# A fourth product-saving inner pair in each gate and up group, hidden tiles split by accumulating DMAs, products in written order

## The chip, the core and the metric

The kernel runs on one core of one Trainium2 chip. The metric is the time of one execution in microseconds (us), measured on the device; a smaller one is better. Short names of the engines: PE is the matrix engine (PEld its weight loads), DVE the vector engine, ACT the scalar engine, POOL the general engine that here only issues transfers, SP the engine that issues the weight loads.

## The reference

One block of a hybrid encoder for 256 rows of width 2048, all in float32: a mixing layer of four groups, a cross attention over 256 memory rows, and a SwiGLU layer. The change is in the last.

```
x = x + mix @ w_out
x = x + cross_attention(rms_norm(x, norm_g[1]), mem_n, w_xq, w_xkv, w_xo)
gate, up = jnp.split(rms_norm(x, norm_g[2]) @ w_gate_up, 2, axis=-1)   # 2048 x 11264
x = x + (silu(gate) * up) @ w_down                                     # 5632 x 2048
return rms_norm(x, final_norm_g)
```

## The kernel before

**Products.** A float32 number is kept as a rounded part (high) and the rest (low), and each product of an activation tile and a weight tile takes three matmuls: high by high, high by low, low by high (`part`, lines 433 to 435; each is 128 rows by 128 by 512 columns). All weights lie in memory as one stream of slabs, 128 partitions by 2048 columns, in the order in which they are used.

**The stream.** `Stream` turns slabs into weight tiles. A plain slab gives two halves of 1024 columns; for each half ACT casts it into `wh` (line 135) and DVE subtracts to get `wl` (line 136). The `wh` and `wl` tiles rotate over four buffers, so a half can be cast once PE has finished the half that came four earlier. Raw slabs rotate over three buffers. `_fill` keeps the making a few halves ahead of the use.

**Seven products for eight.** Two inner tiles (a pair `ks`) by two column blocks, for two row halves, are eight products. A slab in `PAIRED` does them in seven (Winograd's scheme), 21 matmuls for 24: the activations' sums stand in tiles `z` (`combine`, made once and used for all groups), the weights' sums are made for each slab in `_sums`. Such a slab comes in four phases of 1024, 512, 1024 and 1024 columns, which serve 2, 1, 2 and 2 products; each phase has a cast (line 159) and a subtraction (line 160). Phases 2 and 3 (counted from 0) also need sums of the slab's columns. A slab in `SUMMED` has part of its sums made by transfers: two loads on SP and an accumulating one on POOL (line 102) fill a tile `two`, and DVE adds twice (line 157). One that is in `PAIRED` alone has DVE add four times.

**Gate and up.** The 22 column blocks of `w_gate_up` are done in eleven groups of a gate and an up block, 512 columns each, with all sixteen inner tiles `h3`. The first group is plain; each of the other ten walks the string `GROUP`, one letter for a slab: N is a plain slab (24 matmuls), S one of seven products. When the last S of a group is done, `mixed` joins the products on DVE and ACT; when the last N is done, `upped` and `up` finish the group: two additions, two multiplications, two transposes on DVE (line 557), and then POOL stores the result to the tensor `hidden` (line 559) and loads it again, turned, as four tiles of 128 by 256 (line 564). The generator `fetch` splits each loaded tile into high (ACT) and low (DVE) for the down product; `split` stands in a fixed place by `keep_place`, and a tile is split some steps after its load.

**Down.** `down` does `w_down` in two passes with plans of their own; `down_end` does the last twelve inner tiles of the last column block, one row half after the other, after four matmuls with the identity (line 1244) have added earlier sums to the second row half.

**Who sets the order.** The source is emitted in program order. Background generators (`Background.poll`) are run between products while a planned DVE backlog `owed` is small, and `drain` emits what is left of one. A scheduler then places each engine's instructions by its own estimate of when they can run, except where `keep_place` ties an instruction to the one ahead of it on its engine. At run time each engine takes its instructions in that order.

Of the kernel before, what the change touches and what calls it, by code (L numbers as in the profile page):

```python
# [14 lines left out]
F32R = mybir.dt.float32r  # L15
# [4 lines left out]
ALU = mybir.AluOpType  # L20
# [3 lines left out]
P = 128  # L24
R = 256
# [16 lines left out]
LATE = 12  # L42

GATE_UP = 1920 // 16 + 8
GROUP = "NNSNSNSN"

DOWN = GATE_UP + 80
PASSES = "NNNNSNNSNNSNNSNNSNNSNN", "NSNSNSNSNSNSNSNSNSNNNN"

PAIRED = {a + i for a, plan in [(GATE_UP + 8 * j, GROUP) for j in range(10)] + [(DOWN, PASSES[0]), (DOWN + 22, PASSES[1])]  # L50
          for i, x in enumerate(plan) if x == "S"}
SUMMED = {i for i in PAIRED if i < DOWN}

LAG, OWED, SOON, FAR = 1.3, 0.9, 0.01, 18.0
V_NG = 0
# [16 lines left out]
class Stream:  # L72
# [21 lines left out]
    def _load(self, n):  # L94
# [3 lines left out]
        if n // 16 + 1 in SUMMED:  # L98
# [4 lines left out]
            self.two.append(t)  # L103
        if n // 16 in SUMMED:
            nc.sync.dma_start(self.raw[:, 0:1536], self.W[n // 16][:, 0:1536])
# [149 lines left out]
class Block:  # L255
# [42 lines left out]
    def split2(self, hi, lo, src):  # L298
        self.nc.scalar.copy(hi, src)
        self.tt(lo, src, hi.bitcast(F32), ALU.subtract)  # L300

    def gap(self, pool, n):

        pool.tile([P, n // 4], F32, name=f"gap{next(self.kept)}")
# [159 lines left out]
    def paired_rows(self, w, cols, slots, sums, plan, mixed, first, ready=None, late=0, before=None, swap=False):  # L464

        st, s, nk = self.st, len(sums), len(slots)  # L470
        rest = [k for k in range(nk) if not any(k in ks for ks, _ in sums)]
        steps = [(c, k) for c in range(2) for k in rest]
        todo, q = iter(sums), {}
        count = {"a0": len(rest) + s, "a1": len(rest) + s, "b0": len(rest) + s, "b1": len(rest)}
        left, total = {}, 0

        def put(name, hi, lo, wh, wl):
            if name not in q:
                for x in [name] if name in count else "1675":
                    q[x] = (self.bank if (name in count) == swap else self.gbank)()  # L480
                    left[x] = count.get(x, s)
            new = left[name] == count.get(name, s)
            left[name] -= 1
            self.part(q[name][:, :], hi, lo, wh, wl, new, left[name] == 0)

        form = lambda t, r: (t[:, r * P:(r + 1) * P], t[:, R + r * P:R + (r + 1) * P])
        n = done = 0
        for i, kind in enumerate(plan):
            if before:
                before(i)  # L490
            if kind == "S":
                ks, z = next(todo)
                a = [form(slots[ks[0]], 0), form(slots[ks[1]], 0), form(slots[ks[1]], 1)]
                hi, lo, x4 = self.forms(z, slots[ks[0]])
                x1, s2, s3 = ((hi[:, i * P:i * P + P], lo[:, i * P:i * P + P]) for i in range(3))
                t = (("5", x1), ("7", s3))
                pairs = iter((("1", a[0]), ("b0", x4), ("a0", a[1]), *(t if st.n // 16 in SUMMED else t[::-1]), ("a1", a[2]), ("6", s2)))
                for parts in st.take_sums(w, ks, cols):
                    for wh, wl in parts:
                        name, (hi, lo) = next(pairs)  # L500
                        put(name, hi, lo, wh, wl)
                        self.bg.poll()
                done += 1
                if done == s:
                    mixed(*(q[i] for i in "1567"))
            else:
                for c, k in steps[n:n + 4]:
                    if ready:
                        ready(k)
                    wh, wl = st.take(w, k, cols[c], 4)  # L510
                    for r in range(2):
                        put("ab"[c] + str(r), *form(slots[k], r), wh, wl)
                        self.bg.poll()
                n += 4
            if first and done == s and n >= len(rest):
                first(q["a0"], q["a1"])
                first = None
        assert n == len(steps) - late and done == s
        return [q["b0"], q["b1"]], rest[len(rest) - late:]
# [527 lines left out]
    def gate_up(self, gp, f, z):  # L1047

        nc = self.nc
        box, g, stored = {}, {}, []  # L1050

        def gate(ps):
            for r in range(2):
                g[r] = gp.tile([P, 512], F32, name=f"g{r}", tag=f"g{r}")
                nc.scalar.activation(g[r], ps[r], AF.Silu, scale=box["col"][:, r:r + 1])

        def up(j, ps, h=None):
            h = h or [gp.tile([P, 512], F32, name="h", tag="h", bufs=2) for _ in range(2)]
            for r in range(2):
                self.stt(h[r], ps[r], box["col"][:, r:r + 1], g[r], ALU.mult, ALU.mult)  # L1060
                self.store_turned(self.ff, 4 * j, r, g[r], h[r])
            stored.append(self.bg.now)

        def mixed(q1, q5, q6, q7):

            g[0], g[1], h[0], h[1] = (gp.tile([P, 512], F32, name=n, tag=n, bufs=b) for n, b in (("g0", 1), ("g1", 1), ("h", 2), ("h", 2)))
            nc.scalar.copy(g[0], q1)
            self.tt(h[0], g[0], q6, ALU.add)
            self.tt(g[1], h[0], q7, ALU.add)
            self.tt(h[0], q5, h[0], ALU.subtract)  # L1070
            self.tt(h[1], q5, g[1], ALU.subtract)

        def gated(*ps):

            for r in range(2):
                self.tt(g[r], g[r], ps[r], ALU.add)
                nc.scalar.activation(g[r], g[r], AF.Silu, scale=box["col"][:, r:r + 1])

        def upped(j, ps):

            for r in range(2):
                self.tt(h[r], h[r], ps[r], ALU.add)
            up(j, h, h)

        h = {}

        def fetch(k0, k1, ahead, pause, wait=0):

            m = {}
            for k in range(k0, k1 + ahead):  # L1090
                if k < k1:
                    while len(stored) <= k // 4:
                        yield
                    m[k] = self.tmp()
                    self.load_turned(m[k], self.ff, k)
                if k >= k0 + ahead:
                    while wait and self.bg.now < stored[(k - ahead) // 4] + wait:
                        yield
                    mark = self.mark()
                    self.split(f[k - ahead], m.pop(k - ahead))  # L1100
                    self.keep_place(mark)
                    self.have = k - ahead + 1
                    yield pause

        def norm():

            mark = self.mark()
            nc.scalar.activation(self.mg[:, 0:1], self.mg[:, 0:1], AF.Silu)
            self.keep_place(mark)
            yield 2.0  # L1110
            self.row_norm(1, box)
            yield

        arrival = lambda: gp.tile([P, R], F32, name="ar", tag="ar", bufs=4)
        last = self.bg.add(self.arrive(self.xf[1], 3, arrival, self.put3, FAR), go=True)
        col = self.bg.add(norm())

        def combined():
            for ks, z in sums:
                yield 3.0  # L1120
                yield from self.combine(z, *(self.h3[k] for k in ks))

        sums = [((2 * i, 2 * i + 1), z[i]) for i in range(GROUP.count("S"))]
        comb = self.bg.add(combined())
        ps = self.gemm_rows("w_gate_up", [0, DFF], self.h3,
                            parts=[(range(8), [0]), (range(8, 12), [0]), (range(12), [1]), (range(12, 16), [0]), (range(12, 16), [1])],
                            before=lambda n: n in (1, 3) and self.bg.drain(self.late if n == 1 else last))
        self.bg.drain(col)
        gate(ps[0])
        up(0, ps[1])  # L1130
        early = self.bg.add(fetch(0, FT - 22, 3, 2.0, 15))
        self.bg.drain(comb)
        for j in range(1, DFF // 512):
            upped(j, self.paired_rows("w_gate_up", [j * 512, DFF + j * 512], self.h3, sums, GROUP, mixed, gated, swap=j % 2 == 0)[0])
        self.bg.drain(early)
        self.fetch = self.bg.add(fetch(FT - 22, FT, 6, SOON))

    def down(self, f, sp):
# [72 lines left out]
    def down_end(self, f, ss, ps, rest, split):  # L1211
# [29 lines left out]
        mark = self.mark()  # L1241
# [7 lines left out]
        for r in range(2):  # L1249
# [4 lines left out]
            for c in range(3):  # L1254
                x = self.half(c, r)
                self.stt(x, x, 0.375, fg[:, c * 512:(c + 1) * 512], ALU.mult, ALU.mult)
        nc.scalar.mul(fg[:, 3 * 512:4 * 512], fg[:, 3 * 512:4 * 512], 0.375)
        for r in range(2):
            for k, wh, wl in held:
                self.part_rows(ps[r], r, f[k], wh, wl, False, k == FT - 1)  # L1260
            norm(ps[r], r)


# [627 lines left out]
```

## Time and profile before

| | |
|---|---|
| time, median of 3 runs | 1438.75 us (1436.18 to 1439.48) |
| the profiled execution | 1435.07 us, span 1433.3 us, granted clock 0.999 |
| busy, share of the span | PE 99%, PEld 82%, DVE 80%, ACT 57%, POOL 16% |
| matmuls | 6589 recorded |
| transfers | 343.79 MB, mean 240 GB/s |

In the page's rows, "L136" is line 136 of the kernel; "wl<-raw,wh 128x1024" gives the tile written, the tiles read and the shape. In the timeline, the first number is the start in us from the span's start, the second the time of the merged instructions, and the bracket behind tells how long the engine had been idle and what ended that.

### The profile page before, as it was taken

The numbers are of one execution on the slowest core, as the hardware profiler recorded it, in microseconds if no ns is written. First come the engines' busy times: TensorE is split into PE (matmuls) and PEld (weight loads), VectorE is DVE, ScalarE is ACT, GpSimd is POOL, SyncE is SP. The second block draws the span as 40 slices with busy tenths as digits, with TensorE's granted clock in tenths as the row PEclk, the third lists the DMA queues.
The fourth block names the chain that finished last, engine by engine and source line by source line (L and its number), as shares of the span: only waits on it lengthen the run. The fifth ranks groups of instructions, "written<-read, shape, count | busy, mean of one in ns | idle before, by whom it ended". The sixth has DMA issues, their size and how long they took to land.

```text
span 1433.3 us, 18652 instructions
## 1 busy us (share of the span) xinstructions
PE 1423.0 (99%) x6589; PEld 1180.7 (82%) x6589; DVE 1146.2 (80%) x1738; ACT 815.2 (57%) x1183; POOL 234.8 (16%) x306
## 2 busy tenths in 40 slices
PE   9999999999999999999999999999999999999997
PEld 8888888888888888888888888888888888888886
DVE  6667868777877767777677888898888888989997
ACT  7556565446645555556554656555555556655655
POOL 0000100013212223531431121122011002000000
PEclk9999999999999999999999999999999999999999
DMA  9876564546667788964986999889999887655554
GB/s 352 299 285 248 205 206 162 175 169 224 202 196 236 234 267 252 274 200 166 289 239 209 286 286 277 278 275 282 294 293 288 268 260 229 219 230 179 193 218 147
DMA packets 73037, 343.79 MB, mean 240 GB/s; under 512 B 10957, under 2 KB 12654, under 8 KB 45168
## 3 DMA queue, kind: packets, MB, share of 16 engines
q1 hardware_dynamic: 54848, 288.98, 57.5%
q0 software_dynamic: 17664, 52.97, 15.8%
q8 instruction: 51, 0.84, 0.2%
q10 hardware_dynamic: 432, 0.66, 0.1%
q14 instruction: 42, 0.34, 0.1%
HBM read 322.12 MB, written 20.45 MB: 239 GB/s over the span
## 4 chain that ended last, share of the span: by engine, by line
PE 97%; DVE 1%; ACT 0%; DMA 0%; issue 0%; SPq 0%; ACTq 0%
PE pg L433 22%; PE pg L434 22%; PE pg L435 22%; PE pm L434 7%; PE pm L435 7%; PE pm L433 7%; PE pg L381 4%; PE pg L382 2%; PE pm L1344 1%; PE pm L1022 1%; PE pm L993 1%; DMA raw<-in_W 0%; PE pm L1753 0%; DVE res L283 0%; PE pm L994 0%
## 5 line engine op out<-in xcount | busy, mean ns | idle before, releaser
L136 DVE TENSOR_TENSOR wl<-raw,wh 128x1024 fp32r<-128x1024 f32 (+1 forms) x413 | 494.8, 1212 | 166.1 <-ACT wh L135 163.2
L135 ACT CAST wh<-raw 128x1024 fp32r<-128x1024 f32 (+1 forms) x413 | 424.5, 1043 | 283.9 <-PE pg L435 196.4
L433 PE MATMUL pg<-wh,act 128*128 128x512 f32 (+1 forms) x1191 | 465.6, 391 | 0.0
L434 PE MATMUL pg<-wl,act 128*128 128x512 f32 (+1 forms) x1191 | 463.9, 389 | 0.4 <-DVE wl L136 0.2
L435 PE MATMUL pg<-wh,act 128*128 128x512 f32 (+1 forms) x1191 | 463.9, 389 | 0.0
L433 PEld LDWEIGHTS pg<-wh,act 128*128 128x128 f32 x1191 | 223.8, 188 | 47.8 <-issue 1.5
L434 PEld LDWEIGHTS pg<-wl,act 128*128 128x128 f32 x1191 | 223.8, 188 | 47.2 <-DVE wl L136 1.3
L435 PEld LDWEIGHTS pg<-wh,act 128*128 128x128 f32 x1191 | 223.7, 188 | 47.2 <-DVE act L283 0.4
L159 ACT CAST wh<-raw 128x1024 fp32r<-128x1024 f32 (+1 forms) x150 | 137.0, 921 | 146.8 <-DVE raw L157 46.4
L160 DVE TENSOR_TENSOR wl<-raw,wh 128x1024 fp32r<-128x1024 f32 (+1 forms) x150 | 156.1, 1061 | 57.0 <-ACT wh L159 56.8
L434 PE MATMUL pm<-wl,act 128*128 128x512 f32 x309 | 120.5, 390 | 0.1
L433 PE MATMUL pm<-wh,act 128*128 128x512 f32 x309 | 120.2, 389 | 0.0
L435 PE MATMUL pm<-wh,act 128*128 128x512 f32 x309 | 120.2, 389 | 0.0
L381 PE MATMUL pg<-act,wh 128*128 128x512 f32 x256 | 90.5, 395 | 0.0
L382 PE MATMUL pg<-act,wl 128*128 128x256 f32 x256 | 71.8, 280 | 0.0
L434 PEld LDWEIGHTS pm<-wl,act 128*128 128x128 f32 x309 | 58.0, 188 | 13.0 <-DVE wl L136 0.6
L433 PEld LDWEIGHTS pm<-wh,act 128*128 128x128 f32 x309 | 58.0, 188 | 12.0
L435 PEld LDWEIGHTS pm<-wh,act 128*128 128x128 f32 x309 | 58.0, 188 | 12.0
L102 POOL DMA_DIRECT2D two<-in_W x30 | 26.6, 887 | 241.2 <-DMA two<-in_W 116.0
L157 DVE TENSOR_TENSOR raw<-raw 128x512 f32<-128x512 f32 x90 | 62.0, 689 | 1.3
L159 ACT CAST wh<-two 128x1024 fp32r<-128x1024 f32 x30 | 31.6, 1052 | 51.1 <-PE pg L435 21.7
L381 PEld LDWEIGHTS pg<-act,wh 128*128 128x128 f32 x256 | 48.1, 188 | 10.5
(375 smaller groups left out, 1821.9 us busy)
## 6 DMA issues: line engine op xcount, KB each, us to landing
raw<-in_W SPq DMA_DIRECT2D x216, 1024.0 KB, 5.6
raw<-in_W SPq DMA_DIRECT2D x30, 768.0 KB, 6.1
two<-in_W SPq DMA_DIRECT2D x60, 256.0 KB, 4.9
two<-in_W POOLq DMA_DIRECT2D x30, 512.0 KB, 9.3
raw<-in_W SPq DMA_DIRECT2D x11, 512.0 KB, 7.6
hidden<-g POOLq DMA_DIRECT2D x22, 256.0 KB, 3.7
tmp<-hidden POOLq DMA_DIRECT2D x44, 128.0 KB, 5.4
features<-tmp POOLq DMA_DIRECT2D x32, 128.0 KB, 5.3
```

What stands on the lines that cost most here:

```text
L102: nc.gpsimd.dma_start(t, W[:, 512:1536], accum_op=ALU.add)
L135: nc.scalar.copy(wh[:, a:b], r[:, a:b])
L136: nc.vector.tensor_tensor(out=wl[:, a:b], in0=r[:, a:b], in1=wh[:, a:b].bitcast(F32), op=ALU.subtract)
L157: nc.vector.tensor_tensor(out=out, in0=a, in1=b, op=ALU.add)
L159: nc.scalar.copy(wh, src)
L160: nc.vector.tensor_tensor(out=wl, in0=src, in1=wh.bitcast(F32), op=ALU.subtract)
L381: self.nc.tensor.matmul(p[:, :], wh, slot[:, :], start=start, stop=False)
L382: self.nc.tensor.matmul(p[:, 0:R], wl, slot[:, 0:R], start=False, stop=stop)
L433: self.nc.tensor.matmul(p, hi, wh, start=start, stop=False)
L434: self.nc.tensor.matmul(p, hi, wl, start=False, stop=False)
L435: self.nc.tensor.matmul(p, lo, wh, start=False, stop=stop)
L993: nc.tensor.matmul(p[:, :], q[d][:, r * P:(r + 1) * P], kt[d][:, :], start=d == 0, stop=False)
```

## The change

1. `GROUP` becomes `NSNSsNSN`: four of the eight slabs of a group are done in seven products, the second, fourth, fifth and seventh. The fifth, `s`, is not in `SUMMED`: its sums are four DVE additions and no transfers. A fourth tile `z3` holds the sums of the fourth pair of activations.
2. `fetch` uses `split_far`: ACT writes the high part and the negated, rounded source into the low part's place, and an accumulating transfer issued by POOL adds the source. DVE has no part in it. The fixed place (`keep_place`) is gone there.
3. In `paired_rows` and at the end of `down_end` the three matmuls of each product are tied to the order in which they are written.

```diff
-GROUP = "NNSNSNSN"
+GROUP = "NSNSsNSN"
...
-          for i, x in enumerate(plan) if x == "S"}
-SUMMED = {i for i in PAIRED if i < DOWN}
+          for i, x in enumerate(plan) if x in "Ss"}
+SUMMED = {GATE_UP + 8 * j + i for j in range(10) for i, x in enumerate(GROUP) if x == "S"}
...
+    def split_far(self, hi, lo, src):
+
+        self.nc.scalar.copy(hi, src)
+        self.nc.scalar.mul(lo, src, -1.0)
+        self.nc.gpsimd.dma_start(lo, src, accum_op=ALU.add)
...
+            mark = self.mark()
             self.part(q[name][:, :], hi, lo, wh, wl, new, left[name] == 0)
+            self.keep_place(mark)
...
-            if kind == "S":
+            if kind in "Ss":
...
-                    mark = self.mark()
-                    self.split(f[k - ahead], m.pop(k - ahead))
-                    self.keep_place(mark)
+                    t = f[k - ahead]
+                    self.split_far(t[:, 0:R], t[:, R:512], m.pop(k - ahead))
...
-        sums = [((2 * i, 2 * i + 1), z[i]) for i in range(GROUP.count("S"))]
+        z = z + [gp.tile([P, 1024], F32R, name="z3")]
+        sums = [((2 * i, 2 * i + 1), z[i]) for i in range(4)]
...
         for r in range(2):
+            mark = self.mark()
             for k, wh, wl in held:
                 self.part_rows(ps[r], r, f[k], wh, wl, False, k == FT - 1)
+            self.keep_place(mark)
             norm(ps[r], r)
```

## The prediction

> **What bounds the kernel now.** I read the page's first and fourth part, and then the windows of the gate and up groups.
>
> ```profile
> span 1433.3 us, 18652 instructions
> PE 1423.0 (99%) x6589; PEld 1180.7 (82%) x6589; DVE 1146.2 (80%) x1738; ACT 815.2 (57%) x1183; POOL 234.8 (16%) x306
> PE 97%; DVE 1%; ACT 0%; DMA 0%; issue 0%; SPq 0%; ACTq 0%
> 976.00:1018.00 42.00, 42.00 (x187) 34.75 (x187) 36.83 (x45) 24.82 (x31) 7.76 (x9) 1.00 0.93 285
> 1018.00:1059.00 41.00, 41.00 (x182) 33.97 (x181) 35.13 (x40) 22.29 (x26) 7.75 (x9) 1.00 0.91 286
> ```
>
> The chain that ended last is PE's for 97%, and in two windows of a group's length PE is busy for every microsecond (42.00 of 42.00, 41.00 of 41.00). So a matmul less is time less, and any gap that the change opens is time more. DVE is busy 35.13 of 41 us: it has room, but little, and what counts is when in a group it has it.
>
> A group runs from the first matmul of its first slab to that of the next group. These are the two ends of one:
>
> ```profile
> 944.10 0.39 PE L433 MATMUL pg<-wh,act 128*128 128x512 f32 x1
> 985.58 0.39 PE L433 MATMUL pm<-wh,act 128*128 128x512 f32 x1
> ```
>
> It takes 985.58 - 944.10 = 41.48 us for five plain slabs of 24 matmuls and three of 21, which is 183, or 0.2267 us each. A plain slab is then 5.44 us, one of seven products 4.76 us, and its phases 1.36, 0.68, 1.36 and 1.36.
>
> **The matmuls removed.** Four plain slabs and four of 21 make 180: 0.68 us less for each of ten groups, 6.8 us in all. The lists of instructions of the two kernels, as built, have these 30 fewer on PE, so that part of the change is certain.
>
> **What it adds to DVE and ACT.** Slab `s` needs four lows where N had two, and four sums of 128x512.
>
> ```profile
> L136 DVE TENSOR_TENSOR wl<-raw,wh 128x1024 fp32r<-128x1024 f32 x80 | 94.7, 1217 | 5.6 <-ACT wh L135 4.5
> L160 DVE TENSOR_TENSOR wl<-raw,wh 128x512 fp32r<-128x512 f32 x24 | 16.4, 685 | 0.0
> 978.14 3.50 DVE L136 TENSOR_TENSOR wl<-raw,wh 128x1024 fp32r<-128x1024 f32 x3 [0.21 <-ACT wh L135]
> 1393.28 2.87 DVE L157 TENSOR_TENSOR raw<-raw 128x512 f32<-128x512 f32 x4
> 1396.06 1.22 DVE L160 TENSOR_TENSOR wl<-raw,wh 128x1024 fp32r<-128x1024 f32 x1
> 1410.45 0.43 DVE L283 TENSOR_TENSOR tmp<-res,tmp 128x256 fp32r<-128x256 f32 x1
> L159 ACT CAST wh<-raw 128x512 fp32r<-128x512 f32 x24 | 14.9, 620 | 11.9 <-PE pm L435 6.2 <-PE pg L435 5.7
> L135 ACT CAST wh<-raw 128x1024 fp32r<-128x1024 f32 x80 | 81.0, 1048 | 33.0 <-DMA raw<-in_W 12.6 <-PE pg L435 6.6 <-PE pm L435 6.1
> ```
>
> Back to back, three lows take 3.50 us, so one adds (3.50 - 1.22) / 2 = 1.14; four sums hold DVE from 1393.28 to 1396.06, 2.78; a 512 low about 0.60 (the spacing of the sums is 0.7). `s` costs DVE 1.14 + 0.60 + 2.78 = 4.5 us a group more, less 4 x 0.43 = 1.7 where four hidden tiles are split without it: 35.1 + 4.5 = 39.6 of 40.8 us at most. By the average it fits. ACT has 22 of 41 us and gets 1.05 + 0.62 for casts and four negated copies; it fits with ease. The sums of the fourth activation pair are made once, about eight DVE instructions of some 0.43 us, 3.4 us, beside the first group; if nothing covered them they would cost those 3.4.
>
> **The order is the trouble.** I walked one group of the changed kernel through the built order of its instructions, each engine taking its own in turn. Time 0 is the first matmul of slab 1 (N). Rows that it rests on:
>
> ```profile
> 989.98 1.30 DVE L557 STREAM_TRANSPOSE g<-h 128x512 f32<-128x512 f32 x2
> 991.20 1.19 DVE L136 TENSOR_TENSOR wl<-raw,wh 128x1024 fp32r<-128x1024 f32 x1
> 993.51 0.39 PE L435 MATMUL pm<-wh,act 128*128 128x512 f32 x1
> 993.98 1.05 ACT L159 CAST wh<-two 128x1024 fp32r<-128x1024 f32 x1 [1.78 <-issue]
> 1394.80 1.05 ACT L159 CAST wh<-raw 128x1024 fp32r<-128x1024 f32 x1 [2.64 <-DVE raw L157]
> ```
>
> DVE is done with the previous group's sums and transposes at 991.20 - 985.58 = 5.62. A cast into a freed buffer starts some 0.2 us after PE has issued past it (993.98 against 993.74, one matmul after 993.51). PE's second matmul of a half, 0.23 in, is the first to need its low.
>
> *Slab 2 (S).* DVE: low of phase 1 until 6.22, a sum 6.82, low of phase 2 (`two`) 8.04; PE wants that at 5.44 + 1.36 + 0.68 + 0.23 = 7.71, so 0.33 lost, and phase 2 ends at 9.17. On ACT the next cast in the order is half 1 of slab 3, ahead of phase 3 of slab 2, and its buffer is the one that phase 1 holds until 7.48. So that cast runs 7.72 to 8.77, phase 3's until 9.73, and DVE's lows follow in the same order: 9.99 and 11.13. PE wanted phase 3 at 9.40 and gets it at 11.15: 1.75 lost, 2.08 in the slab.
>
> *Slab 4 (S).* Here the hidden tiles come in. In the kernel before, a tile is split three tiles after its load. In the built order of the changed one, the four tiles loaded in a group are split in the same group, and ACT takes all four ahead of the cast of phase 2 of slab 4. It waits for their landing:
>
> ```profile
> 990.99 1.57 POOL L559 DMA_DIRECT2D hidden<-g  x2 [7.62 <-DVE g L557]
> 996.56 3.54 POOL L564 DMA_DIRECT2D tmp<-hidden  x4 [4.00 <-DMA hidden<-g]
> tmp<-hidden POOLq DMA_DIRECT2D x23, 128.0 KB, 5.3
> L291 ACT CAST f<-tmp 128x256 fp32r<-128x256 f32 x14 | 5.6, 401 | 0.0
> 1413.79 0.63 ACT L1257 ACTIVATE raw<-raw 128x512 f32<-128x512 f32 x1 [0.58 <-DMA raw<-in_fg]
> ```
>
> The loads start at 996.56 - 985.58 = 10.98, take 5.3, and follow each other by 3.54 / 4 = 0.885: they land at 16.28, 17.17, 18.05, 18.94. ACT writes a high and a negated copy of the last one (0.40 each; a scaled copy costs what a cast does, 0.63 against 0.62 at 128x512) until 19.75, the cast of phase 2 until 20.8, DVE its low until 22.0. With slab 3 from 12.28 to 17.72, PE wanted it at 17.72 + 1.36 + 0.68 + 0.23 = 19.99: 2.06 lost. Slab 4 ends at 24.54 (17.72 + 4.76 + 2.06), slab 5 so at 24.54 + 4.76 + 2.04 + 0.94 = 32.28 with what follows.
>
> *Slab 5 (`s`), right behind an S.* DVE still has lows of slab 4 and of phases 0 and 1, then the four sums 24.82 to 27.6. Phase 2's cast can start after two of them (1394.80 in the row above lies amid its four sums), but its low has to queue behind the fourth: 28.82. PE wanted it at 24.54 + 2.04 + 0.23 = 26.81: 2.04 lost. Half 0 of slab 6 again goes ahead of phase 3, whose low is done at 31.1 where PE wanted it at 30.21: 0.94 lost. From there to the end of the group I find no gap.
>
> Sum of one such group: 2.08 + 2.06 + 2.04 + 0.94 = 7.1 us of gaps. Groups 1 to 6 split four tiles each and get this; group 7 splits two and gets about 6.4 (its last load lands 1.77 earlier, and part of what slab 4 no longer loses is lost at `s`); groups 8 and 9 split none, so `s` alone loses 1.42 + 0.89 (DVE enters it 0.6 us less behind) and slab 2 its 2.08, 4.4 each; group 10, whose splits wait for buffers instead, I put between the two at 6.0. Together 6 x 7.12 + 6.4 + 2 x 4.4 + 6.0 = 63.9.
>
> **The end of the kernel.**
>
> ```profile
> 1408.35 0.28 PE L1244 MATMUL pm<-tmp,identr 128*128 128x256 f32 x1
> 1410.55 0.77 PE L1244 MATMUL pm<-tmp,identr 128*128 128x256 f32 x2
> 1400.00:1434.00 34.00, 24.54 (x108) 19.55 (x106) 23.85 (x50) 15.86 (x29) 0.00 (x0) 0.93 0.43 155
> ```
>
> Now the four identity matmuls stand among others, of which PE runs 13 while the last of their inputs is made (ready at 1410.45 + 0.43). In the changed order those 13 stand behind them: 13 x 0.2267 = 2.95 us later, with DVE's order there the same.
>
> **Transfers added.** 44 accumulating ones of 128 KB on POOL's queue, POOL idle for over 80% of the span. Nothing but the far later down pass waits for them. For scale:
>
> ```profile
> q0 software_dynamic: 5790, 19.59, 28.2%
> hidden<-g POOLq DMA_DIRECT2D x16, 256.0 KB, 3.7
> two<-in_W POOLq DMA_DIRECT2D x23, 512.0 KB, 9.4
> ```
>
> From the window 851.6 to 1184.1, 332.5 us: 0.282 x 332.5 / 19.59 = 4.8 us of all sixteen transfer engines per MB, so four of them some 2.4 us a group. The share of 0.91 would rise to 0.97 at an unchanged group; a group of 48 us covers it. If that cover is gone (rival A), weights could come up to 2.4 us late a group; I take 0. The queue's order puts the `two` of slab 7 behind the four, which wait for ACT: issued at about 19.75 + 2 x 0.885 = 21.5 it lands 9.4 later, at 31, and slab 7 begins at 32.28 + 5.44 = 37.7, so 0 too; without that cover what is late there comes on top.
>
> **Sum.** -6.8 + 63.9 + 2.95 = +60.0. The profiled execution took 1435.07 us, 3.7 under the median of the runs; on the median the forecast is 1438.75 + 60 = 1498.8, say 1498.
>
> **The rivals.** *A, faster: the feed keeps its lead.* DVE has 1 us a group to spare, and if halves are made early enough that both swapped orders cost under 0.68 us a group and the splits nothing, what is left is -6.8 + 2.95: 1434.9. For it speaks the average, against it that four buffers are all there are and the cast of slab 3 ahead of phase 3 has to wait for PE. 5%.
>
> *B: the order costs, the loads don't.* If the hidden tiles land by about 17 (1.9 us earlier than my 18.94), all ten groups lose 4.4: -6.8 + 44 + 2.95 = +40, 1479. Against it stand the row of 996.56 and 5.3 us. 22%. The Trainium skill, DMA: Bandwidth & Descriptors, "Anatomy of one DMA — SWDGE (gpsimd) path", gives about 2.0 us plus the bytes at 436 GB/s: 2.3 us for 128 KB and 2.6 for 256 KB, an estimate by which they land in time and B holds. The trace does not agree: 5.3 and 3.7 us.
>
> *H: half the order costs.* If ACT and DVE catch up between slabs better than I drew it, half of B's 44 remains: -6.8 + 22 + 2.95, 1457. 6%.
>
> *C: the gaps lower the granted clock.* In the row from 1400 to 1434, PE is busy 24.54 of 34 us and the clock is 0.93. At that clock the 408 us of matmuls in ten groups take 31 more: 1529. Against it: PE would still be busy 85% of a group. 5%. The Trainium skill, TensorE: Matmul & The Clock Gate, "Part 1: The HAM clock gate", has the clock fall after an idle window of some 3.4 us. My longest gap is 2.1, so by that rule C does not come.
>
> The forecast keeps 60%.
>
> **How the numbers follow.** Range 1458 to 1522: it holds the forecast with 10 us either way for transfer times (0.5 us of landing in seven groups is 3.5 us, a phase's low one place off in ten groups 6) and the catch-up that I may have missed, and B. It leaves out A, C and most of H, 15%. About 0.2% is what a measurement of this kernel can tell from no change. Faster 0.05 (A), same 0.02 (between A and H, some 0.4 us a group lost), slower 0.93.
>
> **What would show it.** In the profile of the changed kernel, groups 1 to 6 should last about 48 us and 8 and 9 about 45; PE's gaps should sit ahead of L434 in phases 2 and 3 of slabs 2, 4 and 5, ended by `wl` of L160; ACT should be idle ahead of the hidden tiles' copies, ended by the transfer `tmp<-hidden`; DVE's busy time should hardly change. Before the identity matmuls PE should be idle some 3 us more. If the groups last under 41.5 us, my walk through the queues was wrong as a whole; if slab 4 shows no gap but 2 and 5 do, B holds; if the clock in those windows is under 0.98, C.

## The result, and the profile after

The changed kernel takes 1530.67 us (median of six runs, 1527.24 to 1538.47) against 1436.26 us: the ratio is 1.0662, with a 95% interval of 1.0634 to 1.069. That is 94 us more, where 60 were forecast, and outside the range.

The page of the changed kernel, parts 1 and 4:

```profile
span 1533.3 us, 18733 instructions
PE 1464.1 (95%) x6559; PEld 1191.0 (78%) x6559; DVE 1177.8 (77%) x1762; ACT 847.4 (55%) x1249; POOL 273.1 (18%) x350
PE 76%; DVE 9%; DMA 8%; issue 3%; ACT 2%; POOL 2%; SPq 0%; ACTq 0%; POOLq 0%; DVEq 0%
```

PE has the 30 matmuls less, and yet its busy time went up by 41 us and its idle time from 10 to 69. So there are two losses: gaps, and matmuls that last longer. (A matmul ahead of a gap counts as busy for 0.39 us, in a row it takes 0.2267, so a part of each gap counts as busy too.) The chain names DVE, DMA and ACT where it was PE for 97%.

ACT copies `g` once in each group, near the end of its last slab of seven products, so two neighbouring copies are a group apart. Before, all but one of nine such distances are 41.5 to 41.6 us (41.97 the other). After, from its timeline (start, duration):

```profile
868.77 0.58 ACT L1075 COPY g<-pg 128x512 f32<-128x512 f32 x1
920.23 0.58 ACT L1075 COPY g<-pm 128x512 f32<-128x512 f32 x1
...
1120.19 0.58 ACT L1075 COPY g<-pm 128x512 f32<-128x512 f32 x1
1165.92 0.58 ACT L1075 COPY g<-pg 128x512 f32<-128x512 f32 x1
...
1211.65 0.58 ACT L1075 COPY g<-pm 128x512 f32<-128x512 f32 x1
1273.32 0.58 ACT L1075 COPY g<-pg 128x512 f32<-128x512 f32 x1
```

A group that splits four tiles lasts 51.46 us in the first two rows (five such distances: 50.9 to 52.1). The three groups behind these, of which the first splits two tiles and the others none, last 45.72 to 45.73, the last group 61.67. By the place of the copies, the change costs 7.6 us up to the first one, 81.7 in the nine distances and 10.8 behind them, 100.1 in all, which is the difference of the two profiled spans (the medians differ by 94).

One group's middle, the fourth slab, on PE, ACT and POOL:

```profile
1000.40 0.39 PE L441 MATMUL pg<-wh,act 128*128 128x512 f32 x1
1002.72 0.50 PE L439 MATMUL pm<-wh,z 128*128 128x512 f32 x1 [1.93 <-ACT wh L159]
1003.98 0.80 PE L440 MATMUL pm<-wl,z 128*128 128x512 f32 x1 [0.76 <-DVE wl L160]
1004.58 0.63 PE L441 MATMUL pm<-wh,z 128*128 128x512 f32 x1
...
994.81 0.41 ACT L304 CAST f<-tmp 128x256 fp32r<-128x256 f32 x1 [2.58 <-DMA tmp<-hidden]
996.60 0.41 ACT L304 CAST f<-tmp 128x256 fp32r<-128x256 f32 x1 [1.06 <-DMA tmp<-hidden]
999.46 0.41 ACT L304 CAST f<-tmp 128x256 fp32r<-128x256 f32 x1 [1.61 <-DMA tmp<-hidden]
1001.01 0.40 ACT L304 CAST f<-tmp 128x256 fp32r<-128x256 f32 x1 [0.83 <-DMA tmp<-hidden]
1001.64 1.03 ACT L159 CAST wh<-two 128x1024 fp32r<-128x1024 f32 x1
...
990.26 3.53 POOL L572 DMA_DIRECT2D tmp<-hidden  x4 [2.86 <-DMA hidden<-g]
```

Each of the four tiles holds up ACT until its transfer has landed, the cast of phase 2 (1001.64) comes behind the last, and PE, done at 1000.79, starts again at 1002.72. That is the chain that the prediction walked. What it left at 5% is in the last row of PE: 0.63 us instead of 0.39. From there on, the starts are 0.43 us apart instead of 0.2267. Two windows of the same length, the first from that gap on, the second at about the same place of group 7, which has no gap at slab 4 (the columns are length, busy times, then the granted clock, the share of the transfer engines and GB/s):

```profile
1002.00:1016.00 14.00, 11.50 (x34) 8.48 (x35) 11.80 (x13) 8.04 (x10) 1.70 (x2) 0.76 0.90 205
1108.00:1122.00 14.00, 12.34 (x52) 9.30 (x51) 11.07 (x13) 8.86 (x11) 0.88 (x1) 1.00 0.87 287
```

34 matmuls against 52, and a clock of 0.76 against 1.00. PE's timeline has 120 matmuls of 0.60 us or more (108 of them 0.63), in ten stretches of up to 13: six of them behind slab 4 of groups 1 to 6, two in the last group, one in the down pass and one at the end of the kernel. At 0.43 - 0.23 = 0.2 us each they cost 24 us.

### The profile page after: what moved, and what is told of

Its sections match the earlier page's. It is cut to its first block, busy times and chain, and to the rows that moved or that the text cites. A ratio compares the mean times of both kernels' runs of the same rounds, so it can differ in the third digit from the quotient of the medians.

```text
span 1533.3 us, 18733 instructions
## 1 busy us (share of the span) xinstructions
PE 1464.1 (95%) x6559; PEld 1191.0 (78%) x6559; DVE 1177.8 (77%) x1762; ACT 847.4 (55%) x1249; POOL 273.1 (18%) x350
## 4 chain that ended last, share of the span: by engine, by line
PE 76%; DVE 9%; DMA 8%; issue 3%; ACT 2%; POOL 2%; SPq 0%; ACTq 0%; POOLq 0%; DVEq 0%
PE pg L440 18%; PE pg L441 18%; PE pg L439 18%; PE pm L440 4%; PE pm L441 4%; PE pm L439 4%; PE pg L387 4%; DMA tmp<-hidden 3%; DVE wl L136 3%; DVE wl L160 3%; DMA raw<-in_W 2%; PE pg L388 2%; DMA hidden<-g 1%; ACT wh L135 1%; POOL tmp L572 1%
## 5 line engine op out<-in xcount | busy, mean ns | idle before, releaser
L136 DVE TENSOR_TENSOR wl<-raw,wh 128x1024 fp32r<-128x1024 f32 (+1 forms) x393 | 471.8, 1213 | 167.7 <-ACT wh L135 165.9
L135 ACT CAST wh<-raw 128x1024 fp32r<-128x1024 f32 (+1 forms) x393 | 405.9, 1042 | 280.3 <-PE pg L441 199.4
L440 PE MATMUL pg<-wl,act 128*128 128x512 f32 (+1 forms) x1166 | 457.1, 392 | 8.5 <-DVE wl L160 8.2
L439 PE MATMUL pg<-wh,act 128*128 128x512 f32 (+1 forms) x1166 | 458.3, 393 | 2.1 <-ACT wh L159 1.9
L441 PE MATMUL pg<-wh,act 128*128 128x512 f32 (+1 forms) x1166 | 455.7, 391 | 0.0
L439 PEld LDWEIGHTS pg<-wh,act 128*128 128x128 f32 x1166 | 220.2, 189 | 52.4 <-ACT wh L159 5.1
L159 ACT CAST wh<-raw 128x1024 fp32r<-128x1024 f32 (+1 forms) x190 | 173.8, 923 | 155.1 <-PE pg L441 68.3
L160 DVE TENSOR_TENSOR wl<-raw,wh 128x1024 fp32r<-128x1024 f32 (+1 forms) x190 | 199.1, 1064 | 76.2 <-ACT wh L159 76.0
L441 PEld LDWEIGHTS pg<-wh,act 128*128 128x128 f32 x1166 | 220.1, 189 | 46.0 <-DVE act L283 0.2
L440 PE MATMUL pm<-wl,act 128*128 128x512 f32 x284 | 115.4, 406 | 14.8 <-DVE wl L160 14.8
L439 PE MATMUL pm<-wh,act 128*128 128x512 f32 x284 | 114.7, 404 | 7.4 <-ACT wh L159 7.2
L441 PE MATMUL pm<-wh,act 128*128 128x512 f32 x284 | 113.5, 400 | 0.0
L157 DVE TENSOR_TENSOR raw<-raw 128x512 f32<-128x512 f32 x130 | 89.6, 689 | 2.3
L439 PEld LDWEIGHTS pm<-wh,act 128*128 128x128 f32 x284 | 55.3, 195 | 23.6 <-ACT wh L159 12.0
L441 PEld LDWEIGHTS pm<-wh,act 128*128 128x128 f32 x284 | 55.3, 195 | 11.3
L160 DVE TENSOR_TENSOR wl<-two,wh 128x1024 fp32r<-128x1024 f32 x30 | 36.7, 1224 | 31.8 <-ACT wh L159 31.8
```

What stands on the lines that cost most here:

```text
L135: nc.scalar.copy(wh[:, a:b], r[:, a:b])
L136: nc.vector.tensor_tensor(out=wl[:, a:b], in0=r[:, a:b], in1=wh[:, a:b].bitcast(F32), op=ALU.subtract)
L157: nc.vector.tensor_tensor(out=out, in0=a, in1=b, op=ALU.add)
L159: nc.scalar.copy(wh, src)
L160: nc.vector.tensor_tensor(out=wl, in0=src, in1=wh.bitcast(F32), op=ALU.subtract)
L439: self.nc.tensor.matmul(p, hi, wh, start=start, stop=False)
```

## The experiments

All times are medians in us, beside the kernel before as measured together with them. Distances of two copies of `g` are called group lengths.

**e1, e2, e3: the three parts one at a time.** e1 has the ties of the products alone, e2 the far split alone, e3 the fourth slab alone:

```diff
 e1, on the kernel before
+            mark = self.mark()
             self.part(q[name][:, :], hi, lo, wh, wl, new, left[name] == 0)
+            self.keep_place(mark)
 (and the same around the loop over held)
 e2, on the kernel before
-                    self.split(f[k - ahead], m.pop(k - ahead))
+                    self.split_far(t[:, 0:R], t[:, R:512], m.pop(k - ahead))
 (without its mark and keep_place)
 e3, on the kernel before
-GROUP = "NNSNSNSN"
+GROUP = "NSNSsNSN"
 (with SUMMED, z3 and sums as in the change)
```

> Only the third part of the change: products tied to their written order, the four-slab pattern and the DVE splits as before. Theory Q (the loss is in the queues of ACT and DVE: halves and hidden tiles stand there in an order that PE has to wait for, and a long wait then also lowers the granted clock): the order of ACT and DVE is that of the kernel before, so only the end of the kernel changes, 13 matmuls behind the identity ones: +3 us. Rival O (PE lost the freedom to fill its gaps with other products' matmuls): +20 us or more, with gaps in the gate and up groups.

Measured 1443.79 against 1435.28, ratio 1.0053 (1.0038 to 1.0068): +8 to +9. Theory Q said 3, rival O 20. Some 5 us of it are at the end of the kernel or in the down pass, 2.6 in the groups (the nine distances sum to 376.5 for 373.9).

> Only the second part of the change: hidden tiles split by ACT and an accumulating transfer, three slabs of seven products as before. Theory Q: the tiles loaded in a group are split in the same group, and ACT takes the first one ahead of the halves of the fourth slab; it lands 16.3 us into the group, the halves are wanted at 15.6, so PE waits some 3 us in each of seven groups, and the clock falls behind the wait as in the changed kernel (13 matmuls at 0.43 instead of 0.23 us, 2.6 us): +30 to +45 us. Rival L (the fourth slab's load on DVE is what costs, the far split relieves it): within 3 us of the kernel before, or faster.

Measured 1490.45, ratio 1.0381 (1.0364 to 1.0399): +55. Rival L falls. Theory Q's mechanism is there, but not as regularly as it said: at the fourth slab PE waits 1.2 to 6.2 us in five groups, not seven, and the clock falls in three of them; the size was 10 us over the expected range. PE and ACT of e2, where the fourth slab begins:

```profile
931.42 0.51 PE L439 MATMUL pm<-wh,act 128*128 128x512 f32 x1 [1.92 <-ACT wh L135]
...
930.01 0.40 ACT L304 CAST f<-tmp 128x256 fp32r<-128x256 f32 x1 [3.85 <-DMA tmp<-hidden]
930.33 1.99 ACT L135 CAST wh<-raw 128x1024 fp32r<-128x1024 f32 x2
```

ACT waits 3.85 us for one tile's landing, and the plain half that PE wants stands behind it. Of the 55 us, 37 are in the nine distances (410.8 for 373.9) and 15 behind them; around the end of the last group, where the late tiles' splits stand, PE has gaps of 4.99, 3.37 and 3.06 us.

> Only the first part of the change: four slabs of seven products, hidden tiles split by DVE in a fixed place as before. Theory Q: the second and fifth slab lose 1.4 and 1.0 to 1.6 us a group as in the changed kernel, 24 to 30 us in all, the fourth slab loses nothing, the granted clock stays at 1.00 in the groups; minus 6.8 for the matmuls; the 20 splits come in a crowd at the end of the groups, some 10 us: +27 to +35 us. Rival L: DVE has more to do than in the changed kernel, the groups are no shorter than there: +90 us or more.

Measured 1474.43, ratio 1.0267 (1.0252 to 1.0283): +39. Its groups last 43.7 to 45.1 us. One of them, and PE behind the last one:

```profile
1076.23:1119.89 43.66, 42.63 (x182) 33.31 (x181) 39.37 (x46) 24.33 (x28) 4.21 (x5) 1.00 0.86 257
...
1227.65 0.79 PE L439 MATMUL pg<-wh,f 128*128 128x512 f32 x1 [11.32 <-ACT f L291]
```

DVE is busy 39.4 us of it, more than the kernel before's 35 to 37, but 4 less than the group lasts; the granted clock is 1.00. Theory Q's 2.4 to 3 us a group over the 40.8 of 180 matmuls are there in the last six distances (43.7 to 43.8). Its crowd of splits is, too: of the early 22 tiles the first alone is split in a group, the others stand behind the last one, and PE waits 11.32 us for them at one go; the whole is 4 us over the expected range. Rival L, by its number, falls. The three parts alone sum to 103 us where together they are 94. That the two are near does not show that the parts are independent: the later runs price the same part very differently beside different others.

**e4: gaps by themselves.** Behind the last product of the kernel before stand bursts of 60 matmuls; between two of them ACT copies a tile 0 to 12 times onto itself, and the next burst's first matmul reads it.

```diff
+        for gaps in plan:
+            p = self.bank()
+            for i in range(60):
+                nc.tensor.matmul(p[:, :], (first if i == 0 else a[2])[:, 0:P], a[3][:, :], start=i == 0, stop=i == 59)
+            for g, k in enumerate(gaps):
+                if g:
+                    p = self.bank()
+                    nc.tensor.matmul(p[:, :], a[0][:, 0:P], a[3][:, :], start=True, stop=True)
+                nc.scalar.mul(a[0][:, 0:R], p[:, 0:R], 0.0)
+                for _ in range(k):
+                    nc.scalar.copy(a[0][:, 0:R], a[0][:, 0:R].bitcast(F32))
+            first = a[0]
```

> The kernel before, and behind its last product 55 bursts of 60 matmuls of 128x512, parted by gaps of 0.7 to about 6 us that a chain of ACT copies makes; the last 15 gaps have one matmul amid them. It adds work that the reference does not have. Theory G (a gap by its length lowers the granted clock): bursts behind gaps under a bound run at 0.227 us a matmul throughout, those behind longer ones start with some 13 at 0.43, and the bound lies between 1.4 and 1.9 us. Rival P (the clock fell for another reason, the load of the chip around it): the bursts' speed does not go by the gap ahead of them.

A burst takes 13.9 us, or it takes 15.1 to 16.8, with 5 to 14 matmuls at the lower clock. None of the 18 bursts behind a gap of 1.41 us or less is of the longer kind, 10 of 17 behind gaps of 1.83 to 3.15 us are, and all 9 behind gaps of 4.0 us or more (where one matmul stands amid a gap, its longer part is counted). So rival P falls. Theory G holds for long and short gaps, but its bound is no line. Two bursts behind equal gaps of 1.84 us, the first with the fall and the second without; then two neighbouring windows around each of the two gaps:

```profile
1739.46 0.50 PE L625 MATMUL pm<-act,act 128*128 128x512 f32 x1 [1.84 <-ACT act L632]
1816.31 0.50 PE L625 MATMUL pm<-act,act 128*128 128x512 f32 x1 [1.84 <-ACT act L632]
...
1736.98:1740.39 3.41, 1.57 (x7) 0.98 (x6) 0.00 (x0) 1.60 (x4) 0.00 (x0) 1.00 0.01 2
1740.41:1743.80 3.39, 3.39 (x10) 2.61 (x9) 0.00 (x0) 0.00 (x0) 0.00 (x0) 0.50 0.02 5
1812.08:1815.49 3.41, 2.39 (x11) 1.65 (x9) 0.00 (x0) 0.86 (x3) 0.00 (x0) 1.00 0.00 0
1815.50:1818.90 3.40, 2.59 (x11) 2.17 (x12) 0.00 (x0) 0.73 (x2) 0.00 (x0) 1.00 0.00 0
```

What parts them is the place of the gap. The trace records the granted clock, and all 20 falls in e4 begin at whole multiples of 3.413 us from one another. The windows are such stretches of 3.41 us. The first gap lies in one of them, PE is idle for 1.84 us of it, and the next one runs at 0.50. The second gap is parted by a boundary into 1.02 and 0.82 us, and the clock stays at 1.00. The last section has the count for all runs.

**e5 to e8: the splits in place, the halves in order.** The kernels differ in three things:

```diff
 e5, on the changed kernel
+                    mark = self.mark()
                     self.split_far(t[:, 0:R], t[:, R:512], m.pop(k - ahead))
+                    self.keep_place(mark)
 (and the generator of the early tiles is stepped ahead of slabs 1, 3, 5 and 7)
 e6, on e5: casts, sums and subtractions of the halves in gate and up
+            self.keep_place(mark)
 e7, on e6: the ties of the third part taken out
 e8, on e7
-                    self.split_far(t[:, 0:R], t[:, R:512], m.pop(k - ahead))
+                    self.split(f[k - ahead], m.pop(k - ahead))
```

> The changed kernel, but the hidden tiles' splits (by ACT and an accumulating transfer, as in the change) are tied to a fixed place, one ahead of every second slab, each three tiles after its load. Theory Q: ACT has no landing to wait for, slab 4's wait goes and with it the fall of the clock, groups that split tiles last what groups 8 and 9 of the changed kernel do (45.7 us), group 10 too, the end of the kernel stays: 10 x 4.2 + some 6 = +45 to +52 us against the kernel before, clock 1.00 in the groups. Rival W (ACT's second writing and the accumulating transfers cost by their work, wherever they stand): +80 us or more.

Measured 1508.16, ratio 1.0495 (1.0479 to 1.051): +72. In the groups theory Q holds: they last 44.4 to 47.1 us, the last one 45.73, with no fall of the clock. But 34 of the 72 us lie behind the last copy of `g` (283.1 us for 249.2), where the changed kernel has 10.8; neither theory expected that. PE of e5, in the down pass:

```profile
1277.07 0.80 PE L441 MATMUL pg<-wh,act 128*128 128x512 f32 x1 [5.78 <-DMA act<-tmp]
```

There a tile is split just ahead of its use, and the low part's accumulating transfer is on the path.

> As e5, and in gate and up the casts and subtractions of the weight halves are tied to the order in which they are written, so that half 1 of the next slab no longer goes ahead of phase 3. Theory Q: slab 2's loss of 2.3 us a group goes, slab 5's 2.4 stays in the main, as it comes from the four sums: groups 43 to 43.5 us, +22 to +30 us. Rival S (the sums of `s` are all that counts, the order nothing): as e5.

Measured 1503.17, ratio 1.0463 (1.0433 to 1.0492): +67. The nine distances sum to 409.3 where e5's sum to 410.8, so by its total rival S holds, and the 22 to 30 us of theory Q are far off. The single groups say more. Groups 9 and 10, without splits and at full clock in both, last 44.0 us for e5's 45.7. PE in group 10, four gaps of e5 and then two of e6:

```profile
1196.20 0.50 PE L439 MATMUL pm<-wh,act 128*128 128x512 f32 x1 [0.46 <-ACT wh L159]
1197.65 0.50 PE L440 MATMUL pm<-wl,act 128*128 128x512 f32 x1 [0.95 <-DVE wl L160]
1212.85 0.50 PE L440 MATMUL pg<-wl,z 128*128 128x512 f32 x1 [0.93 <-DVE wl L160]
1215.11 0.50 PE L440 MATMUL pm<-wl,act 128*128 128x512 f32 x1 [0.61 <-DVE wl L160]
...
1199.87 0.50 PE L447 MATMUL pg<-wl,z 128*128 128x512 f32 x1 [1.10 <-DVE wl L164]
1216.44 0.50 PE L447 MATMUL pg<-wl,z 128*128 128x512 f32 x1 [0.93 <-DVE wl L164]
```

With the halves in order, the waits at phase 3 of slabs 2 and 5 (1196.20, 1197.65, 1215.11) are gone; in slab 2 the low of phase 2 comes 1.10 us late instead. That is worth 1.7 us a group, where theory Q said 2.3. It is lost again in groups 7 and 8, in which e6 has a fall of the clock that e5 hasn't (47.8 and 47.3 us for 46.0 and 45.7). The stretch ahead of the first of them, and the next one:

```profile
1076.32:1079.73 3.41, 1.50 (x6) 0.72 (x5) 3.29 (x5) 2.28 (x3) 0.00 (x0) 1.00 0.99 360
1079.74:1083.14 3.40, 3.40 (x9) 2.63 (x10) 3.40 (x4) 2.74 (x3) 0.87 (x1) 0.50 0.59 87
```

No gap there is over 0.97 us, but two of them (0.97 and 0.94) lie in one stretch, 1.91 us of idle time together.

> As e6, but without the third part of the change: the matmuls of a product aren't tied to their order, nor those at the end. Theory Q with what e1 showed (the tie costs 8 us where there is little else to wait for): 8 to 12 us less than e6, +12 to +20 us against the kernel before.

Measured 1493.14, ratio 1.0395 (1.0376 to 1.0414): +57, 10 less than e6. As expected from the tie; the level is e6's.

> As e7, but the hidden tiles are split by DVE as in the kernel before (in the same fixed places). Theory Q: DVE gets 1.7 us a group more in the groups that split tiles, of the 1 to 2 us that it has to spare: 0 to 10 us slower than e7. Rival L (DVE's load sets the group): 1.7 us a group in six groups, so at least 10 us slower than e7.

Measured 1474.42, ratio 1.0261 (1.0246 to 1.0276): +38, 19 us faster than e7. Theory Q allowed e8 to be slower, rival L demanded it; both are wrong. In the groups DVE's splits cost 3.1 us more (408.6 for 405.5), behind them they save 22 (250.9 for 272.9). So the far split, in fixed places, loses where it was not looked for, in the down pass.

**e9 to e12: what keeps a group at 43.6 us.**

```diff
 e9, on e8: no additions for s in gate and up (its products of s are not those of the reference)
+                ops = () if self.made // 16 < DOWN else ((s[2], s[2], s[3]), (s[3], s[1], s[3]), (s[1], s[1], s[2]), (s[0], s[0], s[1]))
 e10, on e8
-GROUP = "NSNSsNSN"
+GROUP = "NSNSSNSN"
 e11, on e8
+GROUP = "SNSNsNSN"
 e12, on e11: the halves' ties taken out
```

> As e8, but the four DVE additions of slab `s` are left out (its second and third half hold unsummed columns). e8's groups without splits last 43.6 us, where 180 matmuls need 40.8. Theory D (DVE is late in places, and the sums are what makes it so): 2.8 us less for DVE in each group, groups without splits 41.0 to 41.6, the kernel 20 to 30 us faster than e8. Rival B (the four buffers: two slabs of seven products side by side free them too late for the casts, whatever DVE does): groups stay within 0.7 us of 43.6, under 8 us faster than e8.

Measured 1453.68, ratio 1.0124 (1.0093 to 1.0156): 21 us faster than e8. Theory D holds in size, not in full: the groups without splits last 42.2 us, not 41.0 to 41.6. One gap is left in each, of 1.28 us in group 9 and 0.92 in group 10, in slab 2. DVE and ACT of e9 just ahead of it:

```profile
1132.38 0.71 DVE L570 STREAM_TRANSPOSE g<-h 128x512 f32<-128x512 f32 x1
1133.02 0.65 DVE L164 TENSOR_TENSOR wl<-raw,wh 128x512 fp32r<-128x512 f32 x1
1133.59 0.68 DVE L161 TENSOR_TENSOR raw<-two,raw 128x512 f32<-128x512 f32 x1
1134.30 0.69 DVE L161 TENSOR_TENSOR raw<-raw 128x512 f32<-128x512 f32 x1
...
1135.11 1.05 ACT L163 CAST wh<-raw 128x1024 fp32r<-128x1024 f32 x1 [4.03 <-DVE raw L161]
```

Phase 3 of slab 2 needs a DVE sum, then ACT's cast, then DVE's low, and the sum stands behind the previous group's transposes. With the first seven-product slab third in the group, as before, there is a plain slab more between the two. That this is why the kernel before has no such gap is argued from the rows; no run parts it from the rest.

> As e8, but the fifth slab's sums come from transfers as those of the other three do: two DVE additions in place of four, and 1 MB more of transfers a group. Theory D: half of e9's gain, 8 to 15 us faster than e8, if the transfers find room (their share is 0.86 in the groups). Rival B: within 5 us of e8. Rival T (the transfers become the bound): slower than e8.

Measured 1496.88, ratio 1.0418 (1.039 to 1.0445): 22 us slower than e8. Theory D's gain isn't seen and rival B falls too. Rival T's sign is right and its reason is not: the transfers' share is 0.88 in e10's groups with splits, 0.86 in e8's. ACT and POOL of e10:

```profile
983.40 0.92 POOL L102 DMA_DIRECT2D two<-in_W  x1 [2.92 <-DVE raw L161]
...
993.67 1.04 ACT L163 CAST wh<-two 128x1024 fp32r<-128x1024 f32 x1 [5.24 <-issue]
```

With two S side by side and two tiles `two`, the accumulating transfer was issued when DVE had freed a tile, it landed 10.1 us later, and ACT's cast of `two` starts 0.14 us behind that; PE waits 2.3 to 3.6 us at that place in seven groups, and there the clock falls.

> As e8, but the pattern is SNSNsNSN, so no two slabs of seven products stand side by side. Theory D: `s` gets the time of a plain slab behind it, which is worth up to 1.2 us a group, but the first S now falls where DVE still joins and transposes the last group's results: -10 to +10 us against e8. Rival B: groups 41 to 42 us, 15 to 25 us faster than e8.

Measured 1480.68, ratio 1.03 (1.0276 to 1.0323): 6 us slower than e8, as theory D has it. Rival B, with its 15 to 25 us of gain, falls.

> As e11, but the halves' casts and subtractions are not tied to their order. By e3 and e8 (1474 both) the tie is worth nothing: within 5 us of e11 by theories D and B alike.

Measured 1473.24, ratio 1.0248 (1.0225 to 1.0271), 7 us less than e11, a little over the 5 allowed. No pattern tried here brings a group with four seven-product slabs under the 41.5 us of three.

**e13 to e15: what is left of the 94 us.** Each takes one thing from the changed kernel. They ran at another time than the result above; the kernel before took 1436.83 beside them, for 1436.26.

```diff
 e13: the late 22 tiles by DVE, in a fixed place
-                    self.split_far(t[:, 0:R], t[:, R:512], m.pop(k - ahead))
+                    if k0 == 0:
+                        self.split_far(t[:, 0:R], t[:, R:512], m.pop(k - ahead))
+                    else:
+                        mark = self.mark()
+                        self.split(t, m.pop(k - ahead))
+                        self.keep_place(mark)
 e14: in down_end
-            self.keep_place(mark)
 e15: in paired_rows
-            self.keep_place(mark)
```

> The changed kernel, but only the first 22 hidden tiles are split by ACT and an accumulating transfer; the other 22 by DVE in a fixed place as before. Theory Q: 16 of those 22 stood amid the last group, where ACT waited for the tiles that they overwrite (61.7 us there for 45.7 in the two groups before); that group falls to 45.7 and the gaps at the start of the down pass go: 16 + 4 = 20 us less than the changed kernel. Rival M (the work of these splits only moves): within 6 us of the changed kernel.

Measured 1514.27 against the changed kernel's 1530.67: 16 us less, 4 under what was expected. The last group falls from 61.67 us to what the others without splits have, as the two copies of `g` in e13 show (1254.29 - 1208.53 = 45.76):

```profile
1208.53 0.58 ACT L1075 COPY g<-pm 128x512 f32<-128x512 f32 x1
1254.29 0.58 ACT L1075 COPY g<-pg 128x512 f32<-128x512 f32 x1
```

At the start of the down pass nothing is won: gaps of 2.34 and 1.53 us are there, ended by ACT's casts of the sums for the down pass (`act<-tmp` of 128x128, L299).

> The changed kernel, but the matmuls at its end aren't tied to their order. The prediction priced that tie at 2.95 us. Theory Q with the clock: gaps of 0.94, 1.13 and 1.45 us go, and with them 13 matmuls at the lower clock (2.6 us): 5 to 7 us less than the changed kernel. Rival N (the tie itself and no clock): 3 us less.

Measured 1525.96: 5 us less. The place in the changed kernel, on PE:

```profile
1502.01 0.38 PE L1252 MATMUL pm<-tmp,identr 128*128 128x256 f32 x1 [0.94 <-ACT tmp L299]
1503.52 0.38 PE L1252 MATMUL pm<-tmp,identr 128*128 128x256 f32 x1 [1.13 <-DVE tmp L283]
1505.35 1.04 PE L1252 MATMUL pm<-tmp,identr 128*128 128x256 f32 x2 [1.45 <-ACT tmp L299]
1506.19 0.63 PE L439 MATMUL pm<-wh,act 128*128 128x512 f32 x1
```

Three gaps, 3.52 us together, and the clock falls behind them (0.63). Theory Q's size fits better than N's 3, but runs of one kernel differ by 8 us here, so these two are not well parted.

> The changed kernel, but the three matmuls of each product in the paired slabs aren't tied to their order. Theory Q with what e3 showed (43.7 us in groups without splits where the changed kernel has 45.7): PE fills part of each wait with other products' matmuls, 2 us a group: 15 to 25 us less than the changed kernel. Rival N (the tie costs what it cost in e1, some 4 us without the end): 3 to 6 us less.

Measured 1514.6: 16 us less, at the low end. Groups 7 to 9 last 43.8 to 46.2 us for 45.73, and the last group 52.6 for 61.67. The groups of four splits stay at 49.5 to 51.3: what PE fills in one place it waits for in the next, as the tiles land when they land.

## Why the prediction was wrong

**The matmuls removed: right.** 30 fewer, 6.8 us; the loss is some fourteen times that.

**The walk through a group: its places right, its total in part by luck.** For a group without splits it gave 45.2 us, against 45.73. Counted on PE from start to start, group 9 loses 2.24 us in slab 2, of which 1.96 at phase 3, and 2.43 in slab 5; the walk had 2.08, of which 1.75 at phase 3, and 2.31. e6 bears out the cause given for phase 3, the next slab's half ahead of it on ACT: with that order mended, these waits are gone (2.24 falls to 1.37, 2.43 to 1.57). e9 bears out the sums of `s`: without them the loss in slab 5 is gone, 1.4 us a group. What the expectation ahead of e6 had wrong is that nothing else would hold up slab 2: with the order mended, the low of phase 2 is late there, and e9's rows show what that slab still waits for: transposes, sum, cast, low.

For a group with four splits the walk gave 47.9 us. The distance is 51.46, of which 13 slow matmuls are 2.6: 48.9 without them. Here two errors cancel. At slab 4, in the group of the rows above, PE loses some 3.3 us from start to start where the walk had 2.06; in slab 5 it loses 1.56 where the walk had 2.98, as no wait is left at phase 2. That the slow matmuls of slab 4 give DVE the time to catch up there is likely, but no run shows it. The wait at slab 4 itself is as it was walked, ACT held by `tmp<-hidden` ahead of the cast of `two`.

**The clock: the step that failed.** It was set aside as rival C, at 5%, because PE is still busy 85% of a group and no gap would be longer than 2.1 us. The gaps at slab 4 are 1.86 to 2.65 us with a second one of 0.51 to 0.91 close behind in groups 1 to 6, and the clock fell after each of the six; by the prediction's own sign, a clock under 0.98, C came (0.76 in the window above). In all, 120 matmuls cost 24 us. Neither reason could have told: a fall goes by the idle time in one stretch of 3.41 us, as the last section shows, not by PE's share of a whole group or by the length of one gap. The fall comes on top of the forecast's gaps, so its price belonged in the sum, as C's 1529 had it. That 1529 lies next to the measured time is luck: C's 31 us were for a clock of 0.93 throughout ten groups, the falls cost 24, four of the ten stretches lie in the last group and behind it, and the rest of the miss is the last group's. The Trainium skill, TensorE: Matmul & The Clock Gate, "Part 1: The HAM clock gate", puts the fall behind an idle window of some 3.4 us. The prediction's dismissal drew on that too, and the runs do not agree: in e4, 10 of 17 gaps of 1.83 to 3.15 us were enough, and in e6 two gaps under 1 us.

**The last group: a term mis-sized.** Put at 6.0 us of gaps (46.8 us in all) "between the two", without a walk. It lasts 61.67, and e13 shows that the late tiles' splits are 15.9 of it. PE and DVE of the changed kernel there:

```profile
1247.39 0.80 PE L440 MATMUL pm<-wl,act 128*128 128x512 f32 x1 [4.85 <-DVE wl L160]
...
1245.78 0.43 DVE L283 TENSOR_TENSOR tmp<-act 128x256 f32<-128x256 f32 x1 [7.24 <-DMA act<-tmp]
1246.12 2.95 DVE L160 TENSOR_TENSOR wl<-raw,wh 128x1024 fp32r<-128x1024 f32 x3
```

The accumulating transfer fills the low part of a hidden tile, and an addition on DVE (made early, for the down pass) reads that tile. It holds DVE for 7.24 us, and the low that PE waits for is queued behind it. The prediction said that nothing but the far later down pass waits for these transfers. Here DVE waits for one in the last group, and in e5 the down pass isn't far: PE itself waits there, 5.78 us at once.

**The end and the product order.** The tie at the end was priced at 2.95 us; e14 puts it at 5 with the clock's fall. The tie of the products in the groups was priced at nothing; e15 puts it at 16 where gaps are to be filled, e1 with both ties at 8 to 9 where there are few.

**Group 7: put at 6.4 us of gaps, it has none from splits** (45.72 us), as its two tiles are split without holding anything up.

The sum, between the two profiled executions: 60 forecast, 24 for the clock, some 10 for the last group beyond its forecast and its own two falls, some 3 for gaps at the start of the down pass that were not forecast (0.76, 1.03 and 1.49 us), 1 us in each of groups 1 to 6, less 1.5 for group 7: 101 to 102 of the 100 us that the spans differ by. Not each of these small terms was tested by itself. Rivals A and H fall with the group lengths, B with ACT's waits for `tmp<-hidden`. That DVE had room by the average was true (39.5 us of 45.7) and told nothing.

## What to carry to other kernels

Where an engine is busy all the time, walk its feeders' queues through one period before counting what they have to spare: here the walk found the places of a group's gaps and their sum to within a microsecond, in part by luck, and the averages gave the wrong sign. Then add up PE's idle time over each 3.4 us of the walk, several short gaps together, and where it comes to 1.6 us or more put the price of a fall of the clock into the sum, not into a rival. A split that goes through a transfer frees DVE, but its instructions wait for landings in the queue of an engine that others need, and in a place where the result is used at once the transfer's time is on the path.

## What the runs showed of the hardware

The clock falls at set times and by PE's idle time ahead of them, not by the length of one gap. The traces of all 17 kernels record 104 falls, and within a trace they all begin at whole multiples of 3.413 us from one another, to 0.002 us (those of groups 1 to 6 are 51.2 us apart, 15 times that). Cut at these times, the 3.413 us ahead of a fall have 1.59 us or more without a matmul, in each of the 104. Of some 7200 such stretches at full clock without a fall behind them (the first 30 us of each span left out), the idlest has 1.92 us. So about half a stretch idle is what brings the fall, and between 1.59 and 1.92 us both were seen. A gap of 1.84 us counts or not by where it lies, as e4's windows show, and two gaps of less than 1 us can count, as e6's show. Most falls last one or two such stretches, 3.41 or 6.83 us, a few three. In the changed kernel one in a group slows some 13 matmuls to 0.43 us, 2.6 us more than at full speed; in the bursts of e4 it costs 1.2 to 2.9.

An accumulating transfer of 128 KB within the core's memory took 6.5 us, not much less than the 7.5 of a hidden tile's load from outside. Transfers of the changed kernel from 800 to 1100 us (count, size, median us to landing):

```profile
tmp<-hidden POOLq DMA_DIRECT2D x24, 128.0 KB, 7.5
f<-tmp POOLq DMA_DIRECT2D x14, 128.0 KB, 6.5
```

The loads of hidden tiles took 5.3 us in the kernel before. In the same stretch now they take 7.5, with 128 KB more on the same queue for each of them.
